# Matmul with layer norm, 2048 x 2048 x 2048: five DMA transposes issued on ScalarE's queue, and the first chunk's pieces in another order

## The chip, the core and the metric

The kernel runs on one core of a Trainium2 chip. The metric is the device time of one execution in microseconds (us), the median of several runs. The core has five engines with a queue each, which run side by side and wait for each other through semaphores: TensorE (PE in the profile, its weight loads PEld), VectorE (DVE), ScalarE (ACT), GpSimd (POOL) and SyncE (SP). A queue is worked off in order: what stands behind a waiting instruction waits too. SP, ACT and POOL can issue DMA transfers; 16 DMA engines carry them. In the DMA view, q1 carries the transfers that SP issues (and would carry ScalarE's under the same kind, "hardware_dynamic"), q0 those of POOL ("software_dynamic"), q8 and q14 the loading of the program itself.

## What is computed

```python
x = np.matmul(a, b)                      # a, b: 2048 x 2048, f32
mean = np.mean(x, axis=-1, keepdims=True)
var = np.var(x, axis=-1, keepdims=True)
normalized = (x - mean) / np.sqrt(var + eps)
return (gamma * normalized + beta).astype(np.float32)
```

## The kernel before

**Tiles.** Rows of `a` are taken 128 at a time (row blocks 0 to 15), the inner dimension in 16 steps of 128 (kt 0 to 15), the columns of `b` in four quarters of 512 (q 0 to 3). One matmul takes a 128 x 128 block of `a`, transposed, as weights and a 128 x 512 block of `b`, both in f16, and adds into one of eight PSUM banks. 16 row blocks x 4 quarters x 16 steps make 1024 matmuls.

**The opening.** The data arrive as f32 over DMA into staging tiles (pool `stg`, six of them), and are cast to f16 by DVE (all of `a`, the first part of `b`) or by ACT (the last 14 pieces of `b`). Until `b` is there, the kernel works on the first R = 5 row blocks together, chunk by chunk (a chunk is KC = 4 steps): whatever piece of `b` has come is used for all five rows. I write b(k,q) for the 512 KB piece with the steps k and k+1 of quarter q. In the very first chunk the pieces are half as large: A0 to A4 are the first 512 columns of the row blocks 0 to 4 (256 KB each), B0 to B3 the steps 0 to 3 of quarter 0.

**Transposing `a`.** For the row blocks 0 to 4 the chunks 0, 1 and 2 are transposed on TensorE (`turn`: four transposes for a row, L252, into PSUM, then a copy to SBUF on ACT, L254). The last chunk (kt 12 to 15) is transposed by DMA instead (`turn_last`, L258): five DMA transposes of 128 x 512 in f16, SBUF to SBUF, whose source is the f16 cast of that chunk. The row blocks 5 to 15 are loaded and cast by POOL's DMA (L340) and transposed by DMA on SP's queue (`turn_ahead`, L346), 128 x 2048 at a time. The trace shows DMA transposes as packets of 256 bytes.

**What sets the order.** The schedule is manual: every engine does its instructions in the order in which the program records them. Around the change the program records, in this order: matmuls of the first chunk; quarters 1 and 2 of chunk 0 (L297); quarter 3 (MAIN) over chunks 0 to 2, with its five accumulators copied out by ACT (`put_aside`, L264); the loop `later` (L352) with the last 14 loads of `b`, their casts on ACT (L205), and the five `turn_last`; then `part(0, ...)`, which runs kt 4 to 11 of quarter 0 and adds each row's accumulator to x on DVE (`add_part`, L268), and `part(1, ...)`, which runs kt 4 to 15 of quarter 1. In `part`, kt 12 to 15 are done row by row, so row 0 needs the first `turn_last` and b(12,1) and b(14,1) at once.

**Two waits that the prediction uses.** The five accumulators of `part(1)` get three banks that are free and two that `add_part` of rows 0 and 1 frees: its matmuls of rows 3 and 4 at kt 4 wait for those two adds. On DVE these adds stand behind the cast of b(6,1).

**DMA semaphores.** The framework gives the DMA transfers of SP and ACT eight semaphores in turn. A transfer waits until the one that had its semaphore before has landed.

Of the kernel before, what the change touches and what calls it, by code (L numbers as in the profile page):

```python
# [16 lines left out]
def kernel(  # L17
# [9 lines left out]
    nc = tc.nc  # L27
# [9 lines left out]
    KC = 4  # L37
    KW = KC * P
    n_kc = n_kt // KC
    R = 5  # L40
# [32 lines left out]
    def bank(name):  # L73
        return psum.tile([P, NB], FP32, tag="ps", name=name)
# [4 lines left out]
    def at(i):  # L79
        return pair[i // 2][:, i % 2]  # L80

    def mm(i, q, kt, first, last):
        if (i, q) not in acc:
            acc[i, q] = bank(f"acc{i}_{q}")
        nc.tensor.matmul(  # L85
            acc[i, q], at(i)[:, kt, :], b16[:, kt, ds(q * NB, NB)],
            start=first, stop=last,
        )
# [71 lines left out]

    arrivals = [("a", 0), ("b", 0)] + [("a", i) for i in range(1, R)]
    arrivals += [("b", k) for k in range(1, KC)]

    a16_of = {}
    fresh = {"st": 0}
# [33 lines left out]
    def load_b2(k, q, cast=nc.vector.tensor_copy):  # L201
        st = stg.tile([P, 2, NB], FP32, tag="st", name=f"stb{q}_{k}")
        nc.sync.dma_start(
            st, b[ds(k * P, 2 * P), ds(q * NB, NB)].rearrange("(t p) n -> p t n", p=P))
        cast(b16[:, k:k + 2, ds(q * NB, NB)], st)  # L205
        return st
# [15 lines left out]
    K3 = n_kt - KC  # L222
# [20 lines left out]
    def filler(n, to=None):  # L243
        for _ in range(n):
            nc.tensor.matmul(warm if to is None else to, zeros[:, 0:P], zeros, start=True, stop=True)  # L245

    def turn(rows, c):
        n = len(rows)
        t_ps = psum.tile([P, n, KC, P], FP16, tag="ps", name=f"tps{rows[0]}_{c}")
        for m, i in enumerate(rows):  # L250
            for j in range(KC):
                nc.tensor.transpose(t_ps[:, m, j, :], a16_of[i, c][:, ts(j, P)], ident)  # L252
        i0 = rows[0]
        nc.scalar.copy(  # L254
            pair[i0 // 2][:, ds(i0 % 2, n), ds(c * KC, KC), :], t_ps)

    def turn_last(i):
        nc.sync.dma_start_transpose(at(i)[:, ds(K3, KC), :], a16_of[i, n_kc - 1])  # L258

    def put_aside(p, q):  # L260
        if xs[p] is None:
            xs[p] = xpool.tile([P, N], FP32, tag="x", name=f"x{p}")
            bnst[p] = stat.tile([P, n_nb, 6], FP32, tag="bnst", name=f"bnst{p}")
        nc.scalar.copy(xs[p][:, ds(q * NB, NB)], acc.pop((p, q)))  # L264
# [15 lines left out]
    filler(1)  # L280
    turn([1], 0)
    filler(2)
    for i in range(2, R):
        turn([i], 0)
        mm(i - 1, 0, 0, True, False)
    for p in range(R - 1):
        mm(p, 0, 1, False, False)
    mm(R - 1, 0, 0, True, False)
    mm(R - 1, 0, 1, False, False)
    for kt in range(2, KC):  # L290
        for p in range(R):
            mm(p, 0, kt, False, kt == KC - 1)
            if kt == KC - 1:
                put_aside(p, 0)


    for q in ASIDE[1:]:  # L297
# [40 lines left out]
    def load_row(i):  # L338
        a16[i] = a16p.tile([P, K], FP16, tag="a16", name=f"a16_{i}")
        nc.gpsimd.dma_start(a16[i], a[ts(i, P), :])  # L340
# [8 lines left out]
    later = [(k, 1) for k in range(2 * KC, n_kt, 2)]  # L349
    later += [(k, 2) for k in range(KC, n_kt, 2)]  # L350
    later += [(k, q) for q in (MAIN, 0) for k in range(K3, n_kt, 2)]
    for n, (k, q) in enumerate(later):  # L352
        for i in range(2 * n, min(2 * n + 2, R)):
            turn_last(i)
        st = load_b2(k, q, nc.scalar.copy)
        if (k, q) in ((n_kt - 2, 2), later[-1]):
            nc.gpsimd.tensor_copy(gate, st[:, 0, 0:1])
        if (k, q) == (n_kt - 2, 2):
            load_row(R)
# [152 lines left out]
```

## Time and profile before

| what | us |
|---|---|
| median of 3 runs (244.06 to 244.17) | 244.14 |
| the profiled execution | 244.29 |
| its span, first to last instruction | 242.2 |
| PE busy | 235.4 (97% of the span) |
| DVE busy | 171.6 (71%) |
| ACT busy | 66.0 (27%) |
| 1024 matmuls L85, counted in the chain that ended last | 91% of the span |
| DMA: 53.28 MB, mean rate | 220 GB/s |
| the five DMA transposes L258, issue on SP's queue | 1.2 to 2.6 each |
| the same, from issue to landing | 5.7 to 7.1 |
| loads of b pieces of 512 KB, from issue to landing, median | 7.1 |
| mean granted TensorE clock | 0.993 of full speed |

The span is what lies between the first and the last instruction; the time is about 2 us longer. PE's busy share is near 1 almost everywhere, and matmuls follow each other every 0.216 us when nothing holds them: gaps larger than that are what can be won or lost in the opening.

### The profile page before, as it was taken

To read this page: it belongs to the slowest core of one execution; us is meant where nothing else is said; L and a number is where in the kernel's file an instruction comes from. 1 tells how busy PE (TensorE), PEld (TensorE's weight loads), DVE (VectorE), ACT (ScalarE), POOL (GpSimd) and SP (SyncE) were. 2 spreads that over 40 slices of the span, in tenths; PEclk is the share of its full clock that TensorE was granted. 3 is DMA by queue.
4 is the path that set the end of the run, shared out by engine and by line. 5 is a ranking of instruction groups with operands and counts; after the bars stand their busy time and mean duration, and the time that the engine had idled before them with its cause. 6 is when DMAs were issued, how large, how long until landed. Compare 5 with 4: busy or idle time off the path is not lost.

```text
span 242.2 us, 2970 instructions
## 1 busy us (share of the span) xinstructions
PE 235.4 (97%) x1117; PEld 107.5 (44%) x1117; DVE 171.6 (71%) x300; ACT 66.0 (27%) x115; POOL 12.5 (5%) x20
## 2 busy tenths in 40 slices
PE   7999999999999999999999999999999999999992
PEld 2444554444444444444444444444444444444441
DVE  1554545606359998999999999998858392946761
ACT  2465443146760013020202103112111121112132
POOL 0000000000120001000000000004500000000000
PEclk9999999999999999999999999999999999999997
DMA  5999999999979999948898978999927145130405
GB/s 123 396 387 387 386 384 374 195 344 387 381 137 203 346 209 180 238 180 185 247 229 225 248 162 293 236 201 186 228 81 183 76 117 145 53 120 1 173 0 173
DMA packets 43909, 53.28 MB, mean 220 GB/s; under 512 B 27124, under 2 KB 27124, under 8 KB 43640
## 3 DMA queue, kind: packets, MB, share of 16 engines
q1 hardware_dynamic: 42312, 47.34, 63.7%
q0 software_dynamic: 1584, 5.77, 14.8%
q8 instruction: 8, 0.13, 0.2%
q14 instruction: 5, 0.04, 0.0%
HBM read 35.67 MB, written 16.78 MB: 217 GB/s over the span
## 4 chain that ended last, share of the span: by engine, by line
PE 94%; DMA 2%; ACT 1%; DVE 1%; issue 0%; DVEq 0%
PE acc L85 91%; DMA st<-in_a_dram 2%; PE tps L252 2%; PE warm L245 1%; ACT x L437 1%; DVE bnst L402 0%; DVE x L268 0%; PE y L425 0%; DVE a16s L186 0%; PE ms_ps L420 0%; ACT mv_last L418 0%; DVE mv_last L417 0%; ACT lead L421 0%; DVEq L268 0%
## 5 line engine op out<-in xcount | busy, mean ns | idle before, releaser
L85 PE MATMUL acc<-b,at 128*128 128x512 f16 x1024 | 223.0, 379 | 0.1
L85 PEld LDWEIGHTS <-at 128*128 128x128 f16 x1024 | 99.8, 98 | 120.2 <-ACT at L254 1.1
L96 DVE BATCH_NORM_STATS2 bnst<-x 128x6 f32<-128x512 f32 x43 | 29.4, 687 | 23.0 <-ACT x L95 23.0
L117 DVE SCALAR_TENSOR_TENSOR x<-x,rstd,beta_b 128x512 f32<-128x512 f32 x62 | 44.4, 756 | 0.6
L111 DVE SCALAR_TENSOR_TENSOR x<-x,mv,gamma_b 128x512 f32<-128x512 f32 x60 | 42.9, 756 | 0.0
L95 ACT COPY x<-acc 128x512 f32<-128x512 f32 x43 | 24.5, 585 | 66.9 <-PE acc L85 66.9
L272 DVE TENSOR_TENSOR x<-acc,x 128x512 f32<-128x512 f32 x20 | 13.6, 678 | 13.6 <-PE acc L85 13.6
L106 ACT ACTIVATE sq<-ve 128x1 f32<-128x1 f32 x15 | 3.0, 203 | 65.2 <-DVE ve L104 65.2
L205 DVE CAST b<-stb 128x1024 f16<-128x1024 f32 x16 | 11.1, 694 | 12.5 <-DMA stb<-in_b_dram 12.5
L205 ACT CAST b<-stb 128x1024 f16<-128x1024 f32 x14 | 14.6, 1045 | 16.8 <-DMA stb<-in_b_dram 16.8
L273 DVE BATCH_NORM_STATS2 bnst<-x 128x6 f32<-128x512 f32 x20 | 13.9, 694 | 0.7
L264 ACT COPY x<-acc 128x512 f32<-128x512 f32 x20 | 10.2, 605 | 7.5 <-PE acc L85 7.5
L254 ACT COPY at<-tps 128x512 f16<-128x512 f16 (+1 forms) x11 | 8.1, 742 | 10.8 <-PE tps L252 10.5
L340 POOL DMA_DIRECT2D a<-in_a_dram x11 | 6.0, 548 | 92.9 <-DMA at<-a 92.1
L245 PE MATMUL warm<-zeros 128*128 128x512 f16 x19 | 7.4, 534 | 1.2 <-DVE zeros L152 1.2
L186 DVE CAST a16s<-st 128x512 f16<-128x512 f32 x8 | 3.4, 428 | 5.9 <-DMA st<-in_a_dram 5.7
L194 DVE CAST a16s<-sta 128x1024 f16<-128x1024 f32 x6 | 4.2, 694 | 4.1 <-DMA sta<-in_a_dram 3.4
L386 POOL TENSOR_SCALAR gb<-gb 1x1024 f32<-1x1024 f32 x2 | 5.6, 2829 | 0.0
L252 PEld LDWEIGHTS <-a16s 128*128 128x128 f16 x60 | 4.0, 100 | 3.6 <-DVE a16s L186 2.2
L252 PE MATMUL tps<-ident,a16s 128*128 128x128 f16 x60 | 5.4, 225 | 0.1
L102 DVE BATCH_NORM_AGGREGATE mv<-bnst 128x2 f32<-128x24 f32 x15 | 4.0, 264 | 0.5
L245 PEld LDWEIGHTS <-zeros 128*128 128x128 f16 x19 | 2.2, 127 | 3.9 <-issue 2.5
(33 smaller groups left out, 26.3 us busy)
## 6 DMA issues: line engine op xcount, KB each, us to landing
stb<-in_b_dram SPq DMA_DIRECT2D x30, 512.0 KB, 7.1
out_dram<-x SPq DMA_DIRECT2D x30, 512.0 KB, 4.3
a<-in_a_dram POOLq DMA_DIRECT2D x11, 512.0 KB, 6.2
sta<-in_a_dram SPq DMA_DIRECT2D x6, 512.0 KB, 6.5
st<-in_a_dram SPq DMA_DIRECT2D x8, 256.0 KB, 6.1
st<-in_b_dram SPq DMA_DIRECT2D x4, 256.0 KB, 6.0
gamma_b<-in_gamma_dram SPq DMA_DIRECT2D x1, 1024.0 KB, 5.5
beta_b<-in_beta_dram SPq DMA_DIRECT2D x1, 1024.0 KB, 8.6
```

The costliest lines, as they stand in the source:

```text
L85: nc.tensor.matmul(acc[i, q], at(i)[:, kt, :], b16[:, kt, ds(q * NB, NB)], start=first, stop=last,)
L95: nc.scalar.copy(xs[i][:, qs], acc[i, q])
L96: nc.vector.bn_stats(bnst[i][:, q, :], xs[i][:, qs])
L111: nc.vector.scalar_tensor_tensor(xs[i][:, qs], xs[i][:, qs], mv[:, 0:1], gamma_b[:, qs], AluOp.subtract, AluOp.mult)
L117: nc.vector.scalar_tensor_tensor(xs[i][:, qs], xs[i][:, qs], rstd, beta_b[:, qs], AluOp.mult, AluOp.add)
L205: cast(b16[:, k:k + 2, ds(q * NB, NB)], st)
L245: nc.tensor.matmul(warm if to is None else to, zeros[:, 0:P], zeros, start=True, stop=True)
L252: nc.tensor.transpose(t_ps[:, m, j, :], a16_of[i, c][:, ts(j, P)], ident)
L254: nc.scalar.copy(pair[i0 // 2][:, ds(i0 % 2, n), ds(c * KC, KC), :], t_ps)
L264: nc.scalar.copy(xs[p][:, ds(q * NB, NB)], acc.pop((p, q)))
L272: nc.vector.tensor_tensor(xs[p][:, qs], acc[p, q], xs[p][:, qs], AluOp.add)
L273: nc.vector.bn_stats(bnst[p][:, q, :], xs[p][:, qs])
```

## The change

There are two parts. First, A4 is loaded after B1 and B2 instead of before B1, and the matmuls of the first chunk are recorded in an order that fits: row 4's transposes come late, and its four matmuls come last. Second, `turn_last` issues its DMA transposes on ScalarE's queue instead of SP's, and all five are recorded ahead of the 14 late loads and their casts, instead of two by two between the first of them.

```diff
-    arrivals = [("a", 0), ("b", 0)] + [("a", i) for i in range(1, R)]
-    arrivals += [("b", k) for k in range(1, KC)]
+    arrivals = [("a", 0), ("b", 0)] + [("a", i) for i in range(1, R - 1)]
+    arrivals += [("b", 1), ("b", 2), ("a", R - 1), ("b", 3)]
...
     def turn_last(i):
-        nc.sync.dma_start_transpose(at(i)[:, ds(K3, KC), :], a16_of[i, n_kc - 1])
+        nc.scalar.dma_start_transpose(at(i)[:, ds(K3, KC), :], a16_of[i, n_kc - 1])
...
-    for i in range(2, R):
+    for i in range(2, R - 1):
         turn([i], 0)
         mm(i - 1, 0, 0, True, False)
+    for p in range(R - 2):
+        mm(p, 0, 1, False, False)
+    for kt in (0, 1):
+        mm(R - 2, 0, kt, kt == 0, False)
+    for p in range(R - 2):
+        mm(p, 0, 2, False, False)
+    turn([R - 1], 0)
+    mm(R - 2, 0, 2, False, False)
     for p in range(R - 1):
-        mm(p, 0, 1, False, False)
-    mm(R - 1, 0, 0, True, False)
-    mm(R - 1, 0, 1, False, False)
-    for kt in range(2, KC):
-        for p in range(R):
-            mm(p, 0, kt, False, kt == KC - 1)
-            if kt == KC - 1:
-                put_aside(p, 0)
+        mm(p, 0, 3, False, True)
+        put_aside(p, 0)
+    for kt in range(KC):
+        mm(R - 1, 0, kt, kt == 0, kt == KC - 1)
+    put_aside(R - 1, 0)
...
-    for n, (k, q) in enumerate(later):
-        for i in range(2 * n, min(2 * n + 2, R)):
-            turn_last(i)
+    for i in range(R):
+        turn_last(i)
+    for k, q in later:
         st = load_b2(k, q, nc.scalar.copy)
```

In the built program the rest stands as it stood: the same 1117 instructions of matmul kind on PE, the same casts, the same waits of `part(0)` and `part(1)` on DVE and ACT. The semaphores of the DMA transfers fall differently: b(6,1) now waits for b(8,0) to land, b(8,1) for A4's last chunk; b(12,1) waits for the first `turn_last` to land, b(14,1) for the second, b(4,2) for the third, b(8,2) for the fourth and b(10,2) for the fifth.

## The prediction

> **What bounds the kernel now.** I read the chain of waits first: 91% of the span is matmul after matmul, so only PE's gaps count. From 55.64 us on there is none until the end.
>
> ```profile
> 46.50 0.69 DVE x L268
> ...
> 47.24 8.36 PE acc L85 x38
> ...
> 55.64 177.59 PE acc L85 x822
> ```
>
> 822 matmuls in 177.59 us are 0.216 us each. The matmul starts in the trace leave three gaps after the warm-up that the change can reach. The timeline shows each (start, length, engine, line, what).
>
> ```profile
> 9.29 0.39 PE L85 MATMUL acc<-b,at 128*128 128x512 f16 x1
> 9.57 0.40 PE L252 MATMUL tps<-ident,a16s 128*128 128x128 f16 x4
> 9.76 0.43 DVE L199 CAST b<-st 128x512 f16<-128x512 f32 x1 [0.24 <-DMA st<-in_b_dram]
> 9.95 4.33 PE L85 MATMUL acc<-b,at 128*128 128x512 f16 x19
> 10.23 3.76 PEld L85 LDWEIGHTS <-at 128*128 128x128 f16 x18 [0.17 <-issue]
> ```
>
> Gap 1, 9.51 to 10.23: PE takes A4's transposes, waits 0.15 for row 3's copy on ACT, does one matmul and waits 0.06 for B1's cast (9.76 + 0.43 = 10.19): 0.28 in all.
>
> ```profile
> 37.67 2.70 SPq L258 DMA_TRANSPOSE at<-a16s  x2
> ...
> 40.47 0.53 SPq L203 DMA_DIRECT2D stb<-in_b_dram  x1
> 41.09 4.46 SPq L258 DMA_TRANSPOSE at<-a16s  x2
> ...
> 42.46 0.69 DVE L205 CAST b<-stb 128x1024 f16<-128x1024 f32 x1 [0.81 <-DMA stb<-in_b_dram]
> 45.29 0.69 DVE L205 CAST b<-stb 128x1024 f16<-128x1024 f32 x1 [2.14 <-DMA stb<-in_b_dram]
> 45.60 0.58 SPq L203 DMA_DIRECT2D stb<-in_b_dram  x1
> 45.90 3.08 DVE L268 TENSOR_TENSOR x<-acc,x 128x512 f32<-128x512 f32 x5
> 46.27 1.20 SPq L258 DMA_TRANSPOSE at<-a16s  x1
> 47.24 8.08 PEld L85 LDWEIGHTS <-at 128*128 128x128 f16 x38 [0.36 <-issue]
> ...
> 54.54 1.04 ACT L205 CAST b<-stb 128x1024 f16<-128x1024 f32 x1 [0.75 <-DMA stb<-in_b_dram]
> 55.64 0.31 PEld L85 LDWEIGHTS <-at 128*128 128x128 f16 x2 [0.32 <-issue]
> ```
>
> Gap 2, 47.00 to 47.24: DVE waits 2.14 us for b(6,1), so the adds that free the banks for rows 3 and 4 of part(1) come late. PE goes on 1.97 us after b(6,1) lands (45.27 to 47.24). Gap 3, 55.44 to 55.64: b(14,1), issued by SP behind the transposes, is cast by ACT until 55.58. The three sum to 0.72 us.
>
> **Part by part.** The deltas are worked out in the profiled execution (244.29 = span 242.16 + 2.13 around it) and added to the median 244.14, 0.15 below it.
>
> *First chunk.* Loads land 0.67 us apart (casts at 8.39, 9.09, 9.76, 10.43, 11.11), so B1's cast moves up to 9.09-9.52, B2's to 9.76-10.19, A4's down to 10.43-10.86. The recorded order then runs: the matmul at 9.29, row 0's kt 1 at 9.57, seven more to 11.29 (row 3's copy was done by 9.95, needed at 10.21), A4's transposes (0.22) to 11.52, one matmul, four with B3 from 11.73 (cast done 11.54), four of row 4 to 13.46. Before, the 16 matmuls from 10.23 ended at 13.69. So 0.23 earlier. ACT's copy of row 4 (0.59 after 11.52) is covered by five matmuls (1.08). Nothing is met at 13.46: b(0,1) is cast by 13.16, and the later pieces come over 3 us before use. But this 0.23 is kept only if gap 2 shrinks too, since there PE is released by b(6,1), not by its own pace.
>
> *Transposes off SP.* Five issues (1.30, 1.35, 1.80, 2.60, 1.20) leave SP; SP's loads b(8,1) to b(14,1) no longer stand behind them. They start when a staging tile and their semaphore come free. b(14,1) waits for the second transpose to land; worked through below, it is cast by about 54.5, over a microsecond before PE wants it in the forecast (55.44 + 0.73). So gap 3 goes: -0.20.
>
> *Transposes on ACT.* ACT is idle from its last put_aside (38.51, now 38.28) to its first cast at 47.77. The issues, at their old 8.25 us in all, end at 46.5. That is hidden: the cast of b(8,1) need only start by 49.6 (PE uses it at 50.69, the cast takes 1.05). By the large transposes the same work, 1.25 of them, would take 4.0 (3.2 each, nothing beside them) to 10.8 us (8.61, beside loads): the end is at 42.3 to 49.1, hidden still, by half a microsecond at worst.
>
> *b(6,1) against the transposes.* This decides. Without a transpose beside it b(6,1) would land at 42.46 + 1.36 (a piece's spacing) + 1.0 = 44.8. The 1.0 is a program fetch, a 16 KB packet on q8 at 42.28 in the trace; a like one at 21.39 made the next piece 1.1 us late. Gap 2 closes if b(6,1) lands by 44.80 (PE would come at 46.77; minus 1.97). Before, it landed at 45.27 with the transposes queued behind it on the same queue. Now they come on another queue and need not wait their turn. First packets follow an issue by 1.95 us (issue 106.99, first packet 108.93) to 4.27 (70.95 and 75.22, beside POOL's loads): from 40.2 to 42.55, I take 41.4. No row shows SP's loads beside ACT's transposes. The nearest is POOL's loads beside SP's transposes. Queue lines of five windows, in order 72-74.5, 75.5-77, 77.5-79, 86.5-88, 94-96 us (packets, MB, share):
>
> ```profile
> q0 software_dynamic: 143, 0.52, 108.6%
> ...
> q0 software_dynamic: 55, 0.22, 89.9%
> q1 hardware_dynamic: 48, 0.01, 6.1%
> ...
> q1 hardware_dynamic: 1535, 0.39, 121.3%
> ...
> q0 software_dynamic: 62, 0.25, 88.3%
> q1 hardware_dynamic: 71, 0.02, 9.2%
> ...
> q0 software_dynamic: 97, 0.40, 103.4%
> ```
>
> Alone the load makes 57 or 48 packets a microsecond, beside transposes 37 or 41: 0.64 to 0.85 of its pace; I take 0.74. Transposes fall from 1023 packets a microsecond to 32 to 47, about one for each packet of the load. At 41.4, 3.4 us of loads are left until 44.8; at 0.74 they take 4.6, so b(6,1) lands at 46.0, 0.73 later than before, and PE resumes 0.73 later. Ends: 0.85 from 42.55 gives 45.2 (-0.07); 0.64 from 40.2 gives 47.4 (+2.1). A small gain here is not excluded: it is the first of these ends.
>
> At one for one with SP's loads (12 packets a microsecond on each DMA engine at full pace, 8.9 at 0.74, so 142 on 16), a transpose of some 544 packets takes 3.8 us: the first lands about 45.7, the second 49.5; b(12,1) and b(14,1) follow their own, land near 51.5 and 53.4, and once SP's queue is empty the rest runs at full pace, all landed by about 54.8. PE needs them at 55.7 to 59.2.
>
> [...]
>
> *Sum:* +0.73 at gap 2 (which swallows the first chunk's 0.23) - 0.20 at gap 3 = +0.53: 244.14 + 0.53 = 244.7. Its own ends, -0.27 and +1.9, give 243.9 to 246.0.
>
> **Rivals.** *Loads first, faster:* ACT's transposes get nothing while SP's queue is full. For: in 72.9 to 75.2 the large transpose got nothing while two POOL loads ran. Against: from 75.2 on it did, and slowed them. Then b(6,1) lands at 44.8, all three gaps close: -0.23 - 0.24 - 0.20 = -0.67, 243.5. It decides if b(6,1) lands by 44.8.
>
> [...]
>
> *ACT held:* the issue on ACT can't end before much of the queued transposes has moved (for: 6.88 and 8.61 us beside loads against 3.2 alone; against: the 49.1 above). From an end after 49.6, ACT's casts bind. At 51.0, b(8,1) is ready at 52.05, 1.36 after PE wants it; the next pieces, each cast in 1.05 for 2.16 of matmuls, cost no more. About +1.4, 245.5.
>
> That the change doesn't do what it says is excluded by the program's order: the five stand on ACT's queue, ahead of its casts.
>
> **How the numbers follow.** About 0.2% (0.49 us) is what a measurement of this kernel can tell from no change. Forecast 0.42 (0.25 of it beyond +0.49, 0.17 within), ACT held 0.18, light share 0.18, loads first 0.22. Slower 0.25 + 0.18 = 0.43, same 0.17 + 0.18 = 0.35, faster 0.22. The range 243.4 to 246.2 takes in the loads-first case below and the forecast's own end above; beyond it lie a long hold on ACT and an unseen gain, about 0.15.
>
> **What would show it.** PE without a gap from 9.57 and the first chunk done 0.23 sooner; 256-byte packets before 42.5 among b(6,1)'s own; the DVE cast of b(6,1) at 46.0 instead of 45.29, and PE's gap after it; the cast of b(8,1) on ACT before 49.6; no gap near 55.4. The forecast is wrong if b(6,1) is cast by 45.3 (then 244.0 or less), or if ACT's first cast starts after 49.6.

## The result, and the profile after

| | before | after |
|---|---|---|
| median of 10 runs each, us | 244.62 (244.06 to 245.75) | 249.23 (246.04 to 250.6) |
| the profiled execution | 244.29 | 249.88 |
| its span | 242.2 | 248.1 |
| PE in the chain that ended last | 94% | 73% |
| DMA in it | 2% | 22% |
| granted TensorE clock, mean | 0.993 | 0.986 |

The change made the kernel slower: by 4.6 us by the medians, and by a ratio of 1.0133 (95% interval 1.0101 to 1.0165), some 3.3 us. The ratio leaves out the executions over 1.5% above the fastest of their kernel; of the changed kernel these are four, the profiled one among them. Milder executions are profiled in 14 and 15 below. The forecast was 244.7 in a range to 246.2. In these ten runs the changed kernel also spreads over 4.6 us, where the kernel before spreads over 1.7; that spread became part of the question.

The chain of waits of the changed kernel, its part from 36 to 75 us (start, length, what):

```profile
36.43 7.57 DMA stb<-in_b_dram
...
44.06 13.67 DMA stb<-in_b_dram
57.73 0.02 issue
57.75 1.05 ACT b L205
58.81 0.04 issue
58.85 16.25 PE acc L85 x74
```

Before, this stretch of the chain was matmuls, but for the DVE add at 46.50. Now it is two loads of `b`, one of 7.6 us and one of 13.7, then ACT's cast, then matmuls. The first is b(4,1); when it has landed, SP issues the second, b(10,1). So until 58.85 PE is no longer the bound; a load is.

The timeline of the changed kernel (start, length, engine, line, what; in brackets the idle time before it and what ended it):

```profile
9.15 0.40 PE L252 MATMUL tps<-ident,a16s 128*128 128x128 f16 x4
9.55 2.17 PE L85 MATMUL acc<-b,at 128*128 128x512 f16 x9
11.55 0.39 PE L252 MATMUL tps<-ident,a16s 128*128 128x128 f16 x4
...
37.87 1.29 ACTq L258 DMA_TRANSPOSE at<-a16s  x1
39.20 8.91 ACTq L258 DMA_TRANSPOSE at<-a16s  x4
44.03 0.69 DVE L205 CAST b<-stb 128x1024 f16<-128x1024 f32 x1 [1.29 <-DMA stb<-in_b_dram]
48.99 0.69 DVE L205 CAST b<-stb 128x1024 f16<-128x1024 f32 x1 [4.27 <-DMA stb<-in_b_dram]
49.60 3.08 DVE L268 TENSOR_TENSOR x<-acc,x 128x512 f32<-128x512 f32 x5
50.34 7.63 PE L85 MATMUL acc<-b,at 128*128 128x512 f16 x27 [3.37 <-DVE x L268]
53.23 1.04 ACT L205 CAST b<-stb 128x1024 f16<-128x1024 f32 x1 [14.68 <-DMA stb<-in_b_dram]
57.75 1.04 ACT L205 CAST b<-stb 128x1024 f16<-128x1024 f32 x1 [3.48 <-DMA stb<-in_b_dram]
58.85 3.52 PE L85 MATMUL acc<-b,at 128*128 128x512 f16 x15 [0.88 <-ACT b L205]
```

Gap 1 is gone (9 matmuls run on from 9.55, 0.06 us lost). The cast of b(6,1), at 45.29 before, starts at 48.99; the adds follow it, and PE comes 1.35 us after the cast's start with the first freed bank and 1.95 with the second (50.94), where the forecast had 1.97. Then the second late load: b(10,1) is cast at 57.75, and PE, after the 27 matmuls that it could do (rows 3 and 4 at kt 4, and kt 5 to 9), stands until 58.85.

Where the 5.9 us of span went, from the starts of the matmuls in the trace, as lost time over 0.216 us for each: PE comes to row 3's matmul at kt 4, where it now stops, at 46.81; before, it came there at 46.78 (+0.03) and stopped one matmul later. Then it loses 3.53 in the wait for b(6,1), 1.64 in the eight slow steps after it, 1.04 in the wait for b(10,1) and 0.12 at 61.2, 6.33 in all, against 0.44 in the gaps 2 and 3 before. That is +0.03 + 6.33 - 0.44 = +5.9.

The DMA view of the changed kernel in three windows, 38.5 to 40.5, 41 to 46 and 46.5 to 48.5 us (packets, MB, share of 16 engines). q1 carries SP's loads, q8 program; the transposes from ScalarE, of the same kind, are not on q1 but on a queue of their own, q10:

```profile
q1 hardware_dynamic: 305, 0.57, 94.9%
...
q1 hardware_dynamic: 392, 0.75, 82.9%
q10 hardware_dynamic: 748, 0.18, 49.0%
q8 instruction: 1, 0.02, 1.4%
...
q10 hardware_dynamic: 286, 0.07, 109.5%
q1 hardware_dynamic: 9, 0.01, 3.2%
```

Alone, the loads move 0.57 MB in 2 us, 0.29 a microsecond. Beside the transposes they move 0.15 a microsecond, and in the third window next to nothing: 9 packets in 2 us, and the transposes hardly move either (143 packets a microsecond, against 1023 alone in the large transposes of the trace before).

### The profile page after: what moved, and what is told of

Its sections match the earlier page's. It is cut to its first block, busy times and chain, and to the rows that moved or that the text cites. A ratio compares the mean times of both kernels' runs of the same rounds, so it can differ in the third digit from the quotient of the medians.

```text
span 248.1 us, 2975 instructions
## 1 busy us (share of the span) xinstructions
PE 236.5 (95%) x1117; PEld 107.6 (43%) x1117; DVE 171.1 (69%) x300; ACT 65.9 (27%) x115; POOL 12.7 (5%) x20
## 4 chain that ended last, share of the span: by engine, by line
PE 73%; DMA 22%; DVE 2%; ACT 1%; issue 0%; SPq 0%
PE acc L85 73%; DMA stb<-in_b_dram 19%; DMA st<-in_b_dram 2%; DVE b L205 1%; ACT x L442 1%; ACT b L205 0%; DVE bnst L407 0%; PE y L430 0%; PE ms_ps L425 0%; SPq L184 0%; ACT mv_last L423 0%; DVE mv_last L422 0%; ACT lead L426 0%; SPq L203 0%
## 5 line engine op out<-in xcount | busy, mean ns | idle before, releaser
L117 DVE SCALAR_TENSOR_TENSOR x<-x,rstd,beta_b 128x512 f32<-128x512 f32 x62 | 43.8, 746 | 0.6
L245 PE MATMUL warm<-zeros 128*128 128x512 f16 x19 | 6.8, 498 | 1.2 <-DVE zeros L152 1.2
```

Source lines behind the costliest of these rows:

```text
L117: nc.vector.scalar_tensor_tensor(xs[i][:, qs], xs[i][:, qs], rstd, beta_b[:, qs], AluOp.mult, AluOp.add)
```

## The experiments

Times are medians; the ratio is to runs of the kernel before on the same chip (244.68 for 1, 2, 3 and 5, 244.41 for 4, 6, 7 and 8, 244.47 for 9 to 12). The column of loads in the table at the end counts the 2048-byte packets that start between 40 and 57 us.

**1. The order alone.** The transposes go back to SP, two by two as before; the first chunk stays as changed.

```diff
-        nc.scalar.dma_start_transpose(at(i)[:, ds(K3, KC), :], a16_of[i, n_kc - 1])
+        nc.sync.dma_start_transpose(at(i)[:, ds(K3, KC), :], a16_of[i, n_kc - 1])
...
-    for i in range(R):
-        turn_last(i)
-    for k, q in later:
+    for n, (k, q) in enumerate(later):
+        for i in range(2 * n, min(2 * n + 2, R)):
+            turn_last(i)
```

> Only the first chunk's new order; the transposes stand on SP's queue, two by two, as before. Theory (the transposes beside SP's loads cost the time): the loss is gone, 243.9 to 244.6, the first chunk ends 0.23 us sooner and PE's gap near 47.2 grows by the same 0.23, since the landing of b(6,1) near 45.3 releases PE there. Rival (the new order of pieces is what costs): 246 or more, with gaps before 20 us.

244.14 us (12 runs), ratio 0.9987 [0.9968, 1.0006]. PE came to its stop at 46.88, but b(6,1) was cast only at 46.26 in the profiled execution, and PE waited 0.73 + 0.38, where 0.24 + 0.23 was expected. The first chunk's order does no harm, and what it wins is, as the forecast says, lost again where b(6,1) releases PE.

**2. The transposes alone.** The kernel before with all five transposes on ScalarE's queue, recorded first; the first chunk as before.

```diff
-        nc.sync.dma_start_transpose(at(i)[:, ds(K3, KC), :], a16_of[i, n_kc - 1])
+        nc.scalar.dma_start_transpose(at(i)[:, ds(K3, KC), :], a16_of[i, n_kc - 1])
...
-    for n, (k, q) in enumerate(later):
-        for i in range(2 * n, min(2 * n + 2, R)):
-            turn_last(i)
+    for i in range(R):
+        turn_last(i)
+    for k, q in later:
```

> Only the transposes on ScalarE's queue, all five first; the first chunk as before. Theory: the whole loss stays, 246 to 251, b(6,1) cast at 48 to 49.5 instead of 45.29, a PE gap of 2.5 to 4 us there and half-pace matmuls after it. Rival (the new order costs): 244.1 or a little less.

246.36 us (4 runs), ratio 1.0082 [1.0062, 1.0103]. b(6,1) was cast at 45.98, not at 48 or later, and five gaps between 46.9 and 57.7 make 2.1 us, the largest of 0.93 at the end. So the loss comes from this part, but 1.7 us of it, not the 4.6 of the whole change.

**3. All five first, on SP.** The changed kernel with `nc.sync` in place of `nc.scalar` in `turn_last`, and nothing else.

> The changed kernel with its five transposes back on SP's queue, all five still ahead of the 14 late loads. Theory (it takes a second queue beside the loads): b(6,1), which is ahead of them in the queue, lands at 45 to 45.5 as before; but b(8,1) is issued behind 8.25 us of transposes, near 46, lands near 51 to 52 and PE waits for its cast from 50.5: a gap of 1.5 to 2.5 there, 245.5 to 247. Rival (the position ahead of the loads costs, not the queue): b(6,1) is cast at 48 to 49 here too, 248 to 250.

246.04 us (6 runs), ratio 1.0064 [1.0039, 1.0089]. Here the loads queue behind the transposes on one queue: b(6,1) is cast at 45.91, b(8,1) at 52.02, and PE waits 1.81 us for it at 51.1. So 1.4 us of loss is to be had without a second queue, by recording the transposes ahead of the loads.

**4. Plain copies in place of the transposes.** On ScalarE's queue, of the same size, in runs of 256 bytes. Left out is the transposing of the last chunk of the first five row blocks.

```diff
+        if c == n_kc - 1:
+            held["a3"] = held["a"]
...
-        nc.scalar.dma_start_transpose(at(i)[:, ds(K3, KC), :], a16_of[i, n_kc - 1])
+        nc.scalar.dma_start(
+            at(i)[:, ds(K3, KC), :], held["a3"][:, :, ts(i % KC, P)])
```

> The changed kernel with five plain DMA copies of 128 x 512 f16 on ScalarE's queue in place of its transposes, in runs of 256 bytes: as many packets of the same size. It leaves out the transposes: chunk 3 of the first five rows is not transposed. Theory (transposing packets and loads hold each other up on the DMA engines): copies share without that, b(6,1) is cast by 45.8, the PE gap there is under 1 us, 243.5 to 245. Rival (any second queue beside SP's loads, or many small packets, costs this): b(6,1) near 48 to 49 as in the changed kernel, 247 to 250.

243.65 us (10 runs), ratio 0.9961 [0.9937, 0.9986]. Its timeline has no gap of PE:

```profile
39.83 20.45 PE L85 MATMUL acc<-b,at 128*128 128x512 f16 x94
40.16 4.34 ACTq L260 DMA_DIRECT2D at<-a16s  x5
...
44.71 0.69 DVE L207 CAST b<-stb 128x1024 f16<-128x1024 f32 x1 [0.69 <-DMA stb<-in_b_dram]
```

94 matmuls in 20.45 us, and b(6,1) cast at 44.71, with the program fetch at 42.42 taking 1018 ns. The copies start at 42.16, the transposes of the changed kernel at 40.97; but those of 8, 9 and 16 start as late (42.16 to 42.30) and lose. The copies do slow the loads. The DMA view from 42.5 to 47 us:

```profile
q1 hardware_dynamic: 460, 0.88, 60.5%
q10 hardware_dynamic: 1944, 0.48, 52.8%
```

That is 102 load packets a microsecond, 0.62 of the 166 from 38.5 to 40.5 (332 in 2 us), and 4.2 packets of the copies for each. But the loads keep moving, and the last copy has landed at 50.24, the last transpose of the changed kernel at 56.95. A second queue with as many bytes in as small packets cost the loads nothing that PE felt. What cost time in the changed kernel is the transposing.

**5. The transposes behind the loads.** New first chunk; on SP again, but recorded after b(14,1).

```diff
-    for i in range(R):
-        turn_last(i)
-    for k, q in later:
+    for n, (k, q) in enumerate(later):
+        if n == 4:
+            for i in range(R):
+                turn_last(i)
```

> The new first chunk, and the five transposes on SP's queue behind b(14,1) instead of in front of it. Theory: no transpose is in flight while b(6,1) to b(14,1) load, so b(6,1) lands by 44.8 and b(14,1) by 51; the gaps near 47.2 and 55.4 close, 243.5 (0.67 less than before); the transposes land between 50 and 55, before PE needs them. Rival (they land late): PE waits for the first of them near 55, 244.5 to 247.

244.16 us (12 runs), ratio 0.9991 [0.9976, 1.0005]. The loads that PE waits for come in order (ACT casts at 46.45, 47.81, 49.12, 50.52); what is left is 0.19 us near 46.6 and 0.13 at 80.5. The expected 243.5 was not reached.

**6. The same, with b(6,1) cast on ACT.** b(6,1) becomes the first of `later`, so that its cast no longer stands ahead of the adds on DVE.

```diff
-    load_b2(KC + 2, 1)
...
-    later = [(k, 1) for k in range(2 * KC, n_kt, 2)]
+    later = [(k, 1) for k in range(KC + 2, n_kt, 2)]
...
-        if n == 4:
+        if n == 5:
```

> As the kernel with the transposes behind b(14,1) on SP's queue, and b(6,1) is cast by ScalarE instead of VectorE, so the adds that free the banks no longer stand behind it. Theory (PE near 47.2 waits for the adds, and those only for the cast ahead of them): no gap there whatever b(6,1) does up to 48, 243.4 to 243.7. Rival: nothing beyond the kernel without this, since b(6,1) already lands in time; equal to it within 0.1 us.

243.89 us (12 runs), ratio 0.9973 [0.9945, 1.0]: PE runs without a gap from 10 to 80 us. It is the fastest version here that does all the work, though its interval reaches to no change, and the time is 0.2 above what was expected.

**7. PE kept busy through the wait.** In the changed kernel, 18 matmuls of zeros stand ahead of row 2's first matmul of `part(1)`, in its own bank.

```diff
+                if (q, kt, p) == (1, k0, 2):
+                    acc[p, q] = bank(f"acc{p}_{q}")
+                    filler(18, acc[p, q])
```

> The changed kernel with 18 matmuls on zeros between the second and the third row's first matmul of part(1), into a bank that is free, so that PE is busy through most of its wait. Theory (part of the loss is TensorE's pace after an idle stretch: 0.43 instead of 0.22 us for some eight matmuls): where the wait is over 3.9 us the fillers cost nothing and the matmuls after it keep 0.216, some 1.4 us won against the changed kernel's like runs: 247 to 248.5. Rival (the pace after the wait has another cause, such as the DMA traffic): half-pace matmuls stay, and the time is as the changed kernel's or later.

249.83 us (4 runs), ratio 1.0195 [1.0147, 1.0244]. The slow matmuls after the wait are gone, but nothing is won: PE then waits 2.17 us at 56.1 for b(10,1), cast at 57.43. Here the slow stretch was not on the way that sets the end; the landing of the loads was.

**8. The program fetch moved.** In the changed kernel each 512-wide filler of the warm-up is cut into four of 128: the same work in time (nine of 512 and 36 of 128 both take 4.02 us at the start), but 45 more matmuls, with their weight loads, on PE, which move the program loading on q8 from 45.91 to 34.39 us.

```diff
-        for _ in range(n):
-            nc.tensor.matmul(warm if to is None else to, zeros[:, 0:P], zeros, start=True, stop=True)
+        w = NB if to is not None else NB // 4
+        for _ in range(n * (NB // w)):
+            nc.tensor.matmul(
+                (warm if to is None else to)[:, 0:w], zeros[:, 0:P], zeros[:, 0:w],
+                start=True, stop=True)
```

> The changed kernel with each 512-wide warm-up matmul of the opening cut into four of 128: 45 more pairs on PE's queue, so its program fetches come some 9 us earlier, near 33 and 60 instead of 42. Theory that the fetch during the transposes is a main part (a stretch of 1.5 to 3 us in which nearly no packet moved): b(6,1) is cast 1 to 2.5 us earlier, 245.5 to 247.5. Rival (the sharing of the two queues alone does it): as the changed kernel, b(6,1) near 49.

246.27 us (10 runs), ratio 1.0071 [1.0046, 1.0096]. b(6,1) is cast at 45.76. Three of the 4.6 us are gone with the fetch. But the loads are starved without it too. The DMA view of this kernel from 43 to 46 us:

```profile
q10 hardware_dynamic: 1340, 0.33, 124.7%
q1 hardware_dynamic: 79, 0.13, 11.4%
```

0.04 MB a microsecond for the loads, a seventh of their pace, while the transposes run at 447 packets a microsecond. It is not always so: from 52.5 to 53.5 of the same execution 179 packets of each start, 0.33 MB of loads, as much as they move alone.

**9. The fetch moved into a later stretch.** As 8, with eight fillers of 64 (`NB // 8`).

> The changed kernel with each 512-wide warm-up filler cut into eight of 64: the program fetch of PE moves earlier by about two and a third times what the cut into four moved it (some 18 us), so one falls near 24 us, where no transpose is on its way, and the next near 50 us (estimated from 69.2 less 18.6), among the five transposes again but behind b(6,1). Fetch theory (a 16 KB fetch among transposes in flight freezes them and the loads): b(6,1) is cast near 45.8 as with the fetch moved to 34, but b(8,1) or b(10,1) comes 1 to 2 us later than there, and the time is 247.3 to 249. Rival (the sharing of the DMA engines alone makes the loss, and where the fetch falls does not matter): no dependence on the place, but then the cut into four should not have gained 3 us either; time 246.3 or, if that gain came from something else that the cut changed in the warm-up, 246.0 to 246.5 again.

246.74 us (4 runs, 246.05 to 250.62), ratio 1.0091 [1.0073, 1.011]. The fetch came at 52.0 (1078 ns). b(6,1) was in good time, the second cast of ACT was not:

```profile
44.66 0.69 DVE L205 CAST b<-stb 128x1024 f16<-128x1024 f32 x1 [0.76 <-DMA stb<-in_b_dram]
49.27 1.05 ACT L205 CAST b<-stb 128x1024 f16<-128x1024 f32 x1 [9.87 <-DMA stb<-in_b_dram]
54.01 1.04 ACT L205 CAST b<-stb 128x1024 f16<-128x1024 f32 x1 [3.70 <-DMA stb<-in_b_dram]
55.11 2.75 PE L85 MATMUL acc<-b,at 128*128 128x512 f16 x12 [1.46 <-ACT b L205]
```

And its DMA view in the microsecond from 52.5 to 53.5 against 1.5 us from 54 to 55.5:

```profile
q1 hardware_dynamic: 17, 0.03, 88.4%
q10 hardware_dynamic: 17, 0.00, 2.2%
...
q1 hardware_dynamic: 259, 0.50, 89.9%
q10 hardware_dynamic: 259, 0.07, 19.7%
```

17 and 17 packets a microsecond where it is 173 and 173 later; with the fetch at 34 (experiment 8) the same window has 179 of each. The standstill follows the fetch. What one costs at this place is bounded by PE's gap, 1.62 us. Another 0.93 us of PE's loss lies near 12 us, in the first chunk: a fetch at 9.29 falls into it, and A4 is cast at 11.67 instead of some 10.6. The time expected, 247.3 to 249, was still too high; b(6,1) came a microsecond sooner than supposed.

**10. The fetch just ahead of the transposes.** As 8, with two fillers of 256 (`NB // 2`).

> The changed kernel with each 512-wide warm-up filler cut into two of 256: the fetch moves by about a third of what the cut into four moved it, from a request near 42.3 to about 39.7 us, still ahead of the first 256-byte packets of the transposes (41 to 42.3). Fetch theory: done before the transposes are on their way, it does no harm; b(6,1) cast 45.8 to 46.3, time 246.0 to 246.8, as with the fetch at 34. Rival (the cut helps by something else in the warm-up, in proportion): a third of the gain, 248.2. If the fetch must be farther away than a few us to be harmless, 247 to 249.

246.56 us (4 runs, 245.32 to 248.95), ratio 1.0105 [1.0039, 1.0171]. The fetch moved less than supposed, to 41.41, and ended at 42.29, 0.09 ahead of the first packet of a transpose. The median is within 0.3 of that of experiment 8, but the profiled execution took 248.95: b(6,1) cast at 47.5, b(10,1) at 56.49 with PE standing 2.36 us. So a large loss doesn't need a fetch among the transposes.

**11. The kernel before with its fetch moved** (the edit of 8).

> The kernel before with each 512-wide warm-up filler cut into four of 128, so that the fetch at 42.28 us (2202 ns there) falls near 34. The prediction gave this fetch 1.0 us of b(6,1)'s delay. If so, b(6,1) is cast about 44.3 to 44.8 instead of 45.29, the gap of 0.24 us near 47 is gone and the time is 0.1 to 0.4 below the kernel before, 243.9 to 244.3. If the fetch is harmless for a load behind transposes on one queue, b(6,1) is cast at 45.3 and the time is the same, 244.4. A later fetch moved onto a large transpose could cost up to 0.7, as it did with the cut into four.

244.16 us (10 runs), ratio 0.9986 [0.9965, 1.0006]. b(6,1) is cast at 44.47 instead of 45.29, and the gaps near 47 and 55 are gone. The 1.0 us that the forecast gave the fetch is borne out as 0.8.

**12. Experiment 2 with its fetch moved** (the edit of 8).

> The kernel before with the transposes on ScalarE's queue, all five first (the experiment of the transposes alone), and the warm-up fillers cut into four: the fetch moves from 43.03 to about 35. There it fell into the transposes too, and the kernel took 246.4. Fetch theory: the time falls, to 245.0 to 246.0, b(6,1) cast 45.0 to 45.7. Sharing alone: it stays at 246.2 to 246.5, b(6,1) at 46.0. The comparison with the changed kernel at the same place of the fetch (246.3) shows what the first chunk's order adds: nothing within 0.4 by the theory.

246.4 us (10 runs, 244.18 to 248.1), ratio 1.0048 [1.001, 1.0086]. The profiled execution took 244.23, b(6,1) cast at 44.9, and has one gap of 0.25. The median stays, as sharing alone would have it; the best executions reach the kernel before. With the fetch at 34 and the transposes on SP's queue (11), ten runs lie between 243.92 and 244.86; so the spread that is left here is put down to the transposes on ScalarE's queue. With the fetch at 34 this kernel and that of experiment 8 (246.27), which has the new first chunk as well, take the same time: the order of the first chunk adds nothing there.

**13 to 16. The changed kernel three times more, and experiment 10 once more,** each with a profile, to see what goes with the spread.

> The changed kernel as it is, one more profiled execution. Fetch theory: the time goes with what the fetch does among the transposes. If the fetch's record stands near 42.4 and is over before the transposes are dense, about 246 to 247; if it comes at 45 to 46 with a stretch of a microsecond or more in which almost no packet starts, 248 to 250.5. Rival (sharing alone, varying from one execution to the next): times from 246 to 250 with no relation to the fetch; what goes with the time is how many packets of the loads start between 40 and 57 us (2173 in the kernel before, 1483 in the profile of after).

> The same kernel again; the same two expectations. Over the three: by the fetch theory each execution over 248 has a fetch at 45 to 46 us, by the rival some do not.

> The same kernel a third time; the same two expectations, with the same numbers for the fetch's place and the count of load packets.

> The kernel with the warm-up fillers cut into two of 256 again, the fetch near 41 us, ahead of the transposes. Fetch theory alone: 246.0 to 246.8, the execution of 248.95 was an exception. Sharing that varies by itself: anything from 245.3 to 249, and the time follows the count of load packets between 40 and 57 us (1378 at 248.95).

| profiled execution | time | fetch at | first transpose packet | cast of b(6,1) | load packets, 40 to 57 |
|---|---|---|---|---|---|
| after | 249.88 | 45.91 | 40.97 | 48.99 | 1483 |
| after, 13 | 249.57 | 46.05 | 41.27 | 48.79 | 1639 |
| after, 14 | 246.97 | 44.76 | 40.73 | 47.37 | 1747 |
| after, 15 | 248.30 | 43.70 | 41.17 | 48.15 | 1693 |
| 7 (zeros in the wait) | 249.67 | 45.59 | 41.65 | 48.60 | 1637 |
| 10 (fetch ahead) | 248.95 | 41.41 | 42.38 | 47.5 | 1378 |
| 16 (the same) | 246.94 | 42.09 | 42.25 | 46.33 | 1862 |
| 9 (fetch late) | 246.67 | 52.00 | 42.16 | 44.66 | 1710 |
| 8 (fetch early) | 245.79 | 34.39 | 42.30 | 45.76 | 2012 |
| 12 (2, fetch early) | 244.23 | 34.40 | 41.83 | 44.9 | 2120 |
| 2 (transposes alone) | 246.05 | 43.03 | 41.74 | 45.98 | 1958 |
| 3 (five first on SP) | 246.47 | 42.75 | 42.16 | 45.91 | 1945 |
| before | 244.29 | 42.28 | 41.68 | 45.29 | 2173 |

The strict form of the fetch theory falls: execution 15 took 248.3 with the fetch at 43.7, and execution 10 took 248.95 with none among the transposes. What goes with the time is how far the loads came: over these thirteen and the executions of 1 and 11 (2179 packets, 244.96; 2421, 243.92), the correlation of time and load packets is -0.92. That describes the loss and doesn't explain it, since loads that land late also hold back those behind them; and 5 and 6, whose transposes stand behind the loads that PE wants first, have few load packets (2091 and 2096) and lose nothing. The fetch remains a likely contributor: the kernels whose profiled executions have it between 43.7 and 46.05 (after with 13 to 15, and 7) have a median of 249.6 over 17 runs, those with it elsewhere (8, 9, and 10 with 16) one of 246.6 over 19. All of the latter have the cut warm-up in common; that the fetch and not the cut makes the difference is argued from 11, where the cut wins 0.3.

The mild execution 14 shows how the loss is made up when b(6,1) is less late:

```profile
47.37 0.69 DVE L205 CAST b<-stb 128x1024 f16<-128x1024 f32 x1 [3.17 <-DMA stb<-in_b_dram]
...
49.31 8.36 PE L85 MATMUL acc<-b,at 128*128 128x512 f16 x38 [0.22 <-DVE x L268]
...
57.24 1.04 ACT L205 CAST b<-stb 128x1024 f16<-128x1024 f32 x1 [0.31 <-DMA stb<-in_b_dram]
58.34 1.89 PE L85 MATMUL acc<-b,at 128*128 128x512 f16 x8 [0.67 <-ACT b L205]
```

PE resumes 1.6 us sooner than in the first profile, doesn't wait for b(10,1), and is stopped by the fourth cast of ACT, b(14,1).

## Why the prediction was wrong

The forecast had the direction, and for a reason that held: b(6,1) comes late and PE waits for it. It had +0.5 us where 4.6 were measured. What failed is the pace that the loads keep beside the transposes, and the loads behind b(6,1), which the sum left out.

**The first chunk: right.** PE runs from 9.55 with 0.06 us lost. From A3's cast to its end the chunk takes 5.04 us where it took 5.29, and so in the other profiles: 5.04 to 5.09 with the new order (but for 9), 5.29 or 5.30 with the old. In this pair of profiles it doesn't show at PE's stop, because the loads came 0.28 later (A3 is cast at 8.67, not 8.39). And the gain is lost there, as was said; experiment 1 shows no loss from the order.

**Transposes off SP: wrong in this kernel.** Gap 3 did not close (0.12 are lost there, at 61.2). b(14,1) was not cast by 54.5; b(10,1) already came at 57.75.

**Transposes on ACT: right.** Their issue ended at 48.11, between the bounds of 42.3 and 49.1. ACT's first cast does start after 49.6, at 53.23, which the forecast named as a sign against it; but the bracket of that cast shows what it waited for, the landing of b(8,1), 5.1 us after the issue was over. The rival of ACT held by the issue is refuted by that line, although its +1.4 came, by accident, nearer to the time than the forecast.

**b(6,1) against the transposes: the step that failed.** The mechanism held: first packets at 40.97 (41.4 was taken), b(6,1) late, PE released behind DVE's adds. That refutes the rival of loads first, which had b(6,1) landed by 44.8. The size did not hold. The step gave the loads 0.74 of their pace, with ends at 0.64 and 0.85 from POOL's loads beside SP's transposes. By its own arithmetic, 44.8 - 40.97 = 3.83 us of loads were left and took 48.97 - 40.97 = 8.0: 0.48. The other three executions of the changed kernel give 0.47, 0.61 and 0.52; with the fetch out of the way, and 43.8 in place of 44.8, experiments 8, 9 and 12 give 0.44, 0.66 and 0.65. So the pace is 0.44 to 0.66, the forecast's lower end, 0.64, lies among the best of them, and it varies from one execution to the next. POOL's loads were the wrong row to lean on: their packets were 4096 bytes long and a third as many.

The light share, 0.18 among the chances, was the case of loads that keep 0.82 of their pace, 244.2 in time. The 0.82 was the author's estimate from the commonest lengths of single packets in the trace before, 84 ns for one of a load and 18 for one of a transpose, taken one for one (84/102); no run shows it as a pace up to b(6,1)'s landing, where the executions above gave 0.44 to 0.66. One packet each is what single stretches show (179 and 179 in experiment 8), not the time as a whole; nor do the copies of experiment 4 go one for one, with 4.2 of their packets for each of the loads, which keep 0.62.

**The loads behind b(6,1): left out of the sum.** The step had the five transposes landed by 54.8 and b(12,1) and b(14,1) near 51.5 and 53.4, and so priced one wait only. (Its 45.7 for the first landing is not 41.4 + 3.8, which is 45.2; the sum doesn't use it.) The transposes landed at 56.95, and b(10,1) set PE's start at 58.85. The two loads were not late in being issued: b(6,1) was issued at 38.41 and b(10,1) at 44.06, and they took 10.6 and 13.7 us to land, where 7.1 was the median before. Experiment 7 shows that in an execution like the profiled one this second wait alone fixes the time: with the slow matmuls removed, the wait grew to fill their place. In the milder ones b(14,1) stops PE (14), or no later load does (15).

**The fetch: priced as a constant.** The forecast added 1.0 us for it to b(6,1)'s landing, which experiment 11 bears out for the kernel before (0.8). Among transposes in flight on a second queue it seems to cost more, as experiments 8 and 9 suggest. In the changed kernel its record stands at 43.7 to 46.05, against 42.42 in experiment 4, whose PE does the same up to there: it seems itself to be held up, though no run here shows when it was asked for.

**What stays open.** Why the loads keep 0.48 of their pace in one execution and 0.61 in the next. Neither the fetch nor the start of the first transpose packet decides it alone. And why the two queues go packet for packet in one microsecond while the loads starve in another. The difference between experiment 2 (246.4) and the whole change (249.2) was not split further: in 2 the fetch ran at 43.03, earlier among the transposes, and with the fetch at 34 in both (12 and 8) there is no difference.

## What to carry to other kernels

Keep DMA transposes out of the stretch in which loads are on the critical path: recorded behind those loads on the same queue they cost nothing here (244.16), while on a second queue, free to run beside them, they cost 1.7 to 4.6 us by the medians, and plain copies in the same place nothing (243.65). When a shared resource is priced, price every load that will cross it, not only the first that is late, and treat a pace read from another kind of transfer as a guess in both directions.

## What the runs showed of the hardware

**With a program fetch among transposes, the DMA engines nearly stood still in several executions.** In the changed kernel, with the fetch at 45.91, 286 transpose packets and 9 others started in the 2 us from 46.5, and 8 in all in the microsecond from 46.7; 256-byte packets, 18 ns otherwise, took up to 2451 ns. Experiment 9 moved such a standstill to 52.5 with the fetch. The kernel before has one too, behind the fetch at 42.28, with its transposes on SP's queue (window, length, busy time and instructions by engine, PE's granted clock, DMA share, GB/s):

```profile
44.00:45.00 1.00, 1.00 (x6) 0.47 (x5) 0.00 (x0) 0.00 (x0) 0.00 (x0) 1.00 0.05 5
```

So such a standstill stood in the trace that the forecast was made from. It doesn't follow each time: in 2, 7 and 14 a fetch fell among the transposes, and the emptiest microsecond up to 57 us still had 97, 44 and 52 packet starts. Long packets also came without a fetch, when the transposes began: up to 1655 ns at 43 us in experiment 10, and 2296 at 48.2 in experiment 6.

**Loads and transposes shared the engines unevenly.** In experiment 8 the loads fell to a seventh of their pace for 3 us without any fetch (0.13 MB from 43 to 46), and six microseconds later kept all of it, packet for packet (0.33 MB and 179 packets each from 52.5 to 53.5).

**PE's granted clock fell to 0.50 where 2.84 to 3.74 us lay between two matmuls.** The changed kernel from 51.0 to 53.4 us and from 53.8 to 57.5 (columns as above):

```profile
51.00:53.40 2.40, 2.40 (x6) 0.78 (x6) 1.68 (x3) 0.17 (x1) 0.00 (x0) 0.50 1.14 297
53.80:57.50 3.70, 3.70 (x19) 1.67 (x18) 0.00 (x0) 0.47 (x1) 0.00 (x0) 1.00 1.08 337
```

Clock 0.50, 0.427 us for a matmul. It came where 3.74, 3.50 and 2.84 us lay between the starts of two matmuls (after, 13, 15) and not where it was 2.58 (10) or 1.91 (14). In each of the three it lasted 3.4 us; in 13 and 15 it set in only 1.2 us after PE had gone on. In 15, the execution with 2.84, no later load stops PE, so there the slow matmuls do cost time: 1.7 us are lost in them, of which at most 0.75 could be had, since b(14,1) is ready at 59.23 and used at 59.98.
